# Seven products in place of eight for the down units of the first and last MLP quarter, with three order edges and other PSUM banks

## The chip, the core and the metric

The kernel runs on one core of a Trainium2 chip. The metric is device time in microseconds for one execution of the whole block. PE is TensorE, DVE VectorE, ACT ScalarE, POOL GpSimd and SP the engine that issues most transfers.

## The reference

One decoder block over a sequence of 512 rows of width 1024, all in float32. A mixer (an SSD scan and a causal pooling, merged by sigmoid gates) comes first; the change is in the MLP behind it, and in the last weights of the merge:

```python
h = rmsnorm(x, norm_mix_w[i]) * (1.0 + scale_m) + shift_m
x = x + gate_m * hybrid_mixer(h, ...)          # ends in (g_ssd * y_ssd + g_pool * y_pool) @ w_out
h = rmsnorm(x, norm_mlp_w[i]) * (1.0 + scale_f) + shift_f
x = x + gate_f * (jnp.square(jax.nn.relu(h @ w_up[i])) @ w_down[i])
return rmsnorm(x, norm_final_w)
```

`w_up` is 1024 x 4096, `w_down` 4096 x 1024.

## The kernel before, in words

**Numbers.** Every operand of a large product is split into a high and a low part in fp32r (`two`, L834: ACT copies the high part, DVE takes the difference), and a product is three matmuls: high x high, high x low, low x high (`mm3` for plain products, L156 to L158; `product` for the others, L873). Weights arrive as raw float32 by a transfer from SP into one of four raw buffers `RL` and are split into the nine buffers `HL`. PE takes the weights as the stationary operand, 128 x 128 at a time, and the activations as the moving one.

**Transposed work.** Activations lie as 8 tiles of 128 features by 512 rows. A unit of weights gives one output tile: 8 x 3 = 24 matmuls over 512 columns, into one PSUM bank.

**Quarters.** The 4096 hidden features are worked in four quarters `q` of 8 tiles. In each, up units make 8 tiles `us` (relu, square, split: `activated`, L1067), and down units add 8 output tiles to the residual `x1` (L1174 or L1190). Order of the jobs: the four first up units of quarter 0 as one job (`up_first`, halves of 256 columns), four single up units (`up_plain`), then for each quarter a job of two down units `down_plain(q, (0, 1))`, the other six, and the up units of the next quarter. The very last job, `last_down`, has three down units and the final norm.

**Pairs.** Two units that share their moving operand are a 2 x 2 block product, and `Pair` (L875) does it with seven block products over 256 columns instead of eight (Strassen's scheme in Winograd's form): 7 x 12 = 84 matmuls of 256 columns in place of 2 x 24 of 512. It needs sums of weight blocks and sums of the moving blocks. The weights: `fetch` loads `ya`, `yb` and `y4` by SP and adds two more blocks by accumulating transfers from POOL (L890, L891); `prepare` and `prepare_rest` make two further sums in a tile `z` by DVE (L904 needs `ya`, L907 needs `yb`) and split all of it: S1 and A11 from `ya`, S2 and S4 from `z`, S3 and A12 from `yb`, A22 from `y4`. The moving operand: `sums` (L839) makes the four T tiles from two activation tiles, in place of nothing for plain units; `SQ` lists the quarters whose activations get them, and which therefore have pairs for down units. Before, `SQ = (1,2)`: quarter 0 has six single down units, quarter 3 two, and their weights come as plain units.

A pair's steps on PE: `lead` or `first` (A11 x B11, with A12 x B21 ahead in `lead`), `open` (S1 x T1 into the bank of c12; ACT copies it aside as `s5`, L952), `middle` (S2 x T2; DVE adds `s5` into c12, L964), `third` (S3 x T3 into the same columns as S2 x T2, so only after L964 has read them; DVE makes the other half of the result, L971), `close` (S4 x B22 into c12, A22 x T4 into the bank `ac`). For an up pair, `close` has ACT read both halves of c (L1072 over 256 columns, twice), and then `ac` (L1072 over 512 columns).

**Banks.** PSUM has eight banks. Single units take from `PU` (banks 2 and 3), pairs take `ac` in turn from `AC` (banks 0 and 1) and c11 and c12 from `BE` (banks 4 to 7). Taking and giving back is first in, first out.

**Order.** `run_jobs` (L985) lists the work: before a job runs, the next job's weights are prepared (`ahead`), and the first part of a pair is opened inside the pair before it. `pump` issues the fetches for as long as raw buffers (and, for a pair, one of two buffers `Y4`) are free. The build then writes each engine's order from that list: an instruction in `tc.high_priority()` is taken earlier when it is ready, others as they become ready by the build's own estimate of time; at run time each engine goes through its order. `tc.issue_after(x)` makes what it encloses come behind `x` on the engine of `x`, with no other wait.

**In front of the MLP.** The merge ends with eight gate units; for each ACT does a sigmoid (L728), DVE two steps (L730, L731), and `split` (L126, L127) makes the operand of the units of `w_out` that follow. The weights of `up_first` are converted by ACT whenever they are there.

Of the kernel before, what the change touches and what calls it, by code (L numbers as in the profile page):

```python
# [13 lines left out]
T = 512  # L14
# [48 lines left out]
def block_kernel(tc, xp, crow, arow, par, adaT, wstart, wz, wx, wpool_in, wgate, wpw, wbs, wbp, wout, wup, wdn, out):  # L63
# [3 lines left out]
    with (  # L67
# [53 lines left out]
        done = [None]  # L121

        def split(src):

            hi, lo = S.get(F32R), S.get(F32R)
            act.copy(hi, src)  # L126
            done[0] = dve.tensor_tensor(lo, src, hi.bitcast(F32), ALU.subtract)  # L127
            return hi, lo
# [596 lines left out]
        for j in range(8):  # L725
            gs = F.get()
            ps = unit(wgate[j], h)
            last = act.activation(gs, ps, AF.Sigmoid)  # L728
            PU.put(ps)
            dve.tensor_tensor(gs, gs, acc[j], ALU.mult)  # L730
            dve.tensor_tensor(gs, gs, merged[j], ALU.add)  # L731
            S.put(acc[j])
            F.put(merged[j])
            mg.append(split(gs))
            F.put(gs)
            if rows:
                ada_next()
        free(h)
# [91 lines left out]
        U.free = U.free[:2]  # L830
        spare, ut = [], []
# [43 lines left out]
        class Pair:  # L875
# [24 lines left out]
            def prepare(self):  # L900
                ya, yb = self.y
                self.a, self.left = {}, {}
                z = Z.get()
                dve.tensor_tensor(z[:, :T], ya[:, :T], ya[:, T:], ALU.add)  # L904
                self.keep(ya, "S1", "A11")
                RL.put(ya)
                dve.tensor_tensor(z[:, T:], z[:, :T], yb[:, T:], ALU.add)  # L907
                self.keep(z, "S2", "S4")
                Z.put(z)
# [51 lines left out]
            def middle(self):  # L961
                self.mul(self.ac[:, :H], "S2", "T2")
                with tc.high_priority():
                    dve.tensor_tensor(self.c12, self.ac[:, :H], self.s5, ALU.add)  # L964
                if not self.led:
                    self.mul(self.c11, "A12", "B21")

            def third(self):
                self.mul(self.ac[:, :H], "S3", "T3")
                with tc.high_priority():  # L970
                    dve.tensor_tensor(self.ac[:, H:], self.ac[:, :H], self.s5, ALU.add)  # L971
                U5.put(self.s5)
# [12 lines left out]
        def run_jobs(jobs):  # L985
# [10 lines left out]
            for n, job in enumerate(jobs):  # L996
# [6 lines left out]

                def rest():
                    if isinstance(after, Pair):
                        after.prepare_rest()
                    pump()

                if isinstance(job, Pair):
# [11 lines left out]
                    job.middle()  # L1021
                    if isinstance(after, Pair):
# [4 lines left out]
                else:  # L1027
# [3 lines left out]
                    ahead()  # L1031
                    job.run()
                    rest()
                    if job.after:
                        job.after()

# [28 lines left out]
        us, h2t, hb, ub, held = [], [], {}, {}, []  # L1065

# [53 lines left out]
        def h2_sums():  # L1120
# [10 lines left out]
            spare.extend([S.get(), S.get()])  # L1131
            U.free += [2, 3]
            quarter = [raws[i // 4][:, i % 4, :].bitcast(F32R) for i in range(8)]
            wide = [HI0.get(F32R) for _ in range(2)]
            quarter += [wide[i // 2][:, i % 2 * T:i % 2 * T + T] for i in range(4)]
            for p in range(3):
                ut.append([quarter[4 * p:4 * p + 2], quarter[4 * p + 2:4 * p + 4]])
# [24 lines left out]
        def down_plain(q, js):  # L1162

            def f(w):
# [3 lines left out]
                ps = [PU.get() for _ in js]  # L1168
                n = len(js)
                order = [(k, i) for k in range(6) for i in range(n)] + [(k, i) for i in range(n) for k in (6, 7)]  # L1170
# [6 lines left out]
                PU.put(*ps)  # L1177
# [37 lines left out]
        SQ = (1,2)  # L1215
        jobs = [Plain([Unit(wup[i // 2], i % 2, HI0 if i < 2 else None) for i in range(4)], up_first)]
        jobs += [up_plain(p, i) for p in (2, 3) for i in range(2)]
        jobs[-1].after = h2_sums
# [88 lines left out]
```

## Time and profile before

| | |
|---|---|
| median of 3 runs | 965.71 us (964.55 to 969.83) |
| profiled execution | 964.54 us |
| its span | 962.8 us |
| granted TensorE clock, mean | 0.998 |
| PE busy | 944.3 us, 98% |
| weight loads busy (PEld) | 808.8 us, 84% |
| DVE, ACT, POOL busy | 682.1, 524.0, 121.1 us |
| transfers | 143.43 MB, 149 GB/s over the span |

The span runs from the first to the last instruction; the time lies around it. Matmuls overlap in the records, each from its start to its modelled end, so a busy PE says less than the distance from one start to the next. A row of the timeline gives start, duration, engine, line, operation, tiles (written<-read), how many, and in brackets the idle time before it with what ended it.

### The profile page before, as it was taken

To read this page: it belongs to the slowest core of one execution; us is meant where nothing else is said; L and a number is where in the kernel's file an instruction comes from. 1 tells how busy PE (TensorE), PEld (TensorE's weight loads), DVE (VectorE), ACT (ScalarE), POOL (GpSimd) and SP (SyncE) were. 2 spreads that over 40 slices of the span, in tenths; PEclk is the share of its full clock that TensorE was granted. 3 is DMA by queue.
4 is the path that set the end of the run, shared out by engine and by line. 5 is a ranking of instruction groups with operands and counts; after the bars stand their busy time and mean duration, and the time that the engine had idled before them with its cause. 6 is when DMAs were issued, how large, how long until landed. Compare 5 with 4: busy or idle time off the path is not lost.

```text
span 962.8 us, 13939 instructions
## 1 busy us (share of the span) xinstructions
PE 944.3 (98%) x5347; PEld 808.8 (84%) x5347; DVE 682.1 (71%) x1034; ACT 524.0 (54%) x855; POOL 121.1 (13%) x127
## 2 busy tenths in 40 slices
PE   8999999999999999999999999999999999999996
PEld 4877888888888888788888878997899999899986
DVE  7978868467766787977576574783458878877544
ACT  6479975657528542563312452684147638646633
POOL 0102321220212132300000000000111120111000
PEclk9999999999999999999999999999999999999999
DMA  9846334433253334546578454042556676677402
GB/s 364 303 133 188 125 98 121 131 110 110 79 159 114 98 99 132 158 153 205 181 255 273 130 198 130 23 132 86 133 126 173 147 192 150 179 176 158 148 1 88
DMA packets 69350, 143.43 MB, mean 149 GB/s; under 512 B 5346, under 2 KB 30178, under 8 KB 69283
## 3 DMA queue, kind: packets, MB, share of 16 engines
q1 hardware_dynamic: 64096, 133.09, 43.4%
q0 software_dynamic: 5184, 9.44, 6.6%
q8 instruction: 42, 0.69, 0.3%
q14 instruction: 26, 0.20, 0.1%
q10 hardware_dynamic: 2, 0.00, 0.0%
HBM read 140.29 MB, written 2.23 MB: 148 GB/s over the span
## 4 chain that ended last, share of the span: by engine, by line
PE 79%; DVE 10%; ACT 4%; DMA 4%; issue 2%; POOL 0%; SPq 0%; DVEq 0%; ACTq 0%; POOLq 0%
PE ps L156 19%; PE ps L157 19%; PE ps L158 19%; PE ps L873 14%; PE ps L328 4%; DVE d L147 1%; PE ps L549 1%; DMA d<-cs_d 1%; DVE s L127 1%; DMA d<-wup 1%; DMA d<-wdn 1%; PE ps L529 1%; DVE pad L631 1%; DVE d L172 1%; ACT d L146 1%
## 5 line engine op out<-in xcount | busy, mean ns | idle before, releaser
L156 PE MATMUL ps<-s,d 128*128 128x512 f32 (+1 forms) x984 | 375.1, 381 | 2.4 <-ACT s L126 0.9
L157 PE MATMUL ps<-s,d 128*128 128x512 f32 (+1 forms) x984 | 371.3, 377 | 0.2 <-DVE s L127 0.2
L158 PE MATMUL ps<-s,d 128*128 128x512 f32 (+1 forms) x984 | 371.3, 378 | 0.0
L156 PEld LDWEIGHTS ps<-s,d 128*128 128x128 f32 x984 | 184.6, 188 | 41.2 <-issue 2.4
L158 PEld LDWEIGHTS ps<-s,d 128*128 128x128 f32 x984 | 184.7, 188 | 34.7 <-issue 0.2
L157 PEld LDWEIGHTS ps<-s,d 128*128 128x128 f32 x984 | 184.8, 188 | 33.7 <-DVE s L127 0.5
L147 DVE TENSOR_TENSOR d<-d,d 128x1024 fp32r<-128x1024 f32 x88 | 112.7, 1281 | 61.4 <-ACT d L146 56.4
L146 ACT CAST d<-d 128x1024 fp32r<-128x1024 f32 x88 | 92.0, 1046 | 114.7 <-PE ps L157 74.1
L837 DVE TENSOR_TENSOR d<-d,d 128x1024 fp32r<-128x1024 f32 x82 | 99.6, 1223 | 63.8 <-PE ps L157 36.3
L873 PE MATMUL ps<-s,d 128*128 128x256 f32 x1134 | 139.7, 280 | 2.5 <-DVE ps L964 2.5
L873 PEld LDWEIGHTS ps<-s,d 128*128 128x128 f32 x1134 | 136.2, 188 | 3.4 <-DVE ps L964 3.1
L836 ACT CAST d<-d 128x1024 fp32r<-128x1024 f32 x82 | 85.7, 1049 | 79.6 <-PE ps L158 55.5
L172 DVE CUSTOM_DVE_ANT_0 d<-d,d,par_t 128x1024 f32<-128x1024 f32 x32 | 41.7, 1306 | 27.4 <-DMA d<-adaT 27.4
L890 POOL DMA_DIRECT2D d<-wup x12 | 10.6, 881 | 289.4 <-DMA d<-wup 277.9
L499 ACT ACTIVATE d<-d,ncs 128x128 f32<-128x128 f32 x128 | 39.9, 391 | 4.1 <-POOL d L495 4.0
L328 PE MATMUL ps<-s,d 128*128 128x512 f32 x168 | 40.2, 392 | 1.9 <-ACT s L316 1.9
L397 DVE SCALAR_TENSOR_TENSOR s<-ps,par_t,s 128x511 f32<-128x511 f32 (+2 forms) x54 | 39.7, 742 | 0.3
L328 PEld LDWEIGHTS ps<-s,d 128*128 128x128 f32 x168 | 31.4, 188 | 9.6 <-ACT s L316 2.4
L126 ACT CAST s<-s 128x512 fp32r<-128x512 f32 x32 | 19.7, 619 | 31.2 <-POOL s L511 18.8
L495 POOL TENSOR_SCALAR_AFFINE_SELECT d<-d 128x1024 f32<-128x1024 f32 x16 | 18.2, 1139 | 87.9 <-ACT cd L492 39.9
L127 DVE TENSOR_TENSOR s<-s,s 128x512 fp32r<-128x512 f32 x32 | 25.7, 806 | 4.5 <-ACT s L126 4.3
L511 POOL TENSOR_TENSOR s<-s,dec 128x512 f32<-128x512 f32 x12 | 14.8, 1234 | 90.0 <-issue 55.2
(230 smaller groups left out, 1126.5 us busy)
## 6 DMA issues: line engine op xcount, KB each, us to landing
d<-adaT SPq DMA_DIRECT2D x32, 512.0 KB, 4.1
d<-wup SPq DMA_DIRECT2D x32, 512.0 KB, 5.1
d<-wdn SPq DMA_DIRECT2D x32, 512.0 KB, 4.7
d<-wx SPq DMA_DIRECT2D x18, 512.0 KB, 3.6
d<-cs_d SPq DMA_DIRECT2D x16, 512.0 KB, 6.1
d<-wbs SPq DMA_DIRECT2D x16, 512.0 KB, 3.5
d<-wgate SPq DMA_DIRECT2D x16, 512.0 KB, 4.3
d<-wz SPq DMA_DIRECT2D x15, 512.0 KB, 3.5
```

The lines of the kernel that those rows point to most:

```text
L146: act.copy(hi[:, :w], r[:, a:a + w])
L147: (low or dve).tensor_tensor(lo[:, :w], r[:, a:a + w], hi[:, :w].bitcast(F32), ALU.subtract)
L156: pe.matmul(ps, whi, xhi[:, t0:t1], start=start, stop=False)
L157: pe.matmul(ps, whi, xlo[:, t0:t1], start=False, stop=False)
L158: pe.matmul(ps, wlo, xhi[:, t0:t1], start=False, stop=stop)
L172: dve.tensor_tensor_reduce(r, r, cbc, 1.0, col("b_ada", j), ALU.mult, ALU.add, mod[:, j:j + 1])
L328: pe.matmul(first[u], w[u][i // 2], h[k][i % 2], start=k == 0 and i == 0, stop=k == 7 and i == 2)
L397: dve.scalar_tensor_tensor(t[:, sh:], ps[:, :T - sh], w(3 - sh), t[:, sh:], ALU.mult, ALU.add)
L499: act.activation(m[:, i, :], m[:, i, :], AF.Exp, bias=ncs[:, c, g * HG + i:g * HG + i + 1])
L836: act.copy(dst[0], src)
L837: dve.tensor_tensor(dst[1], src, dst[0].bitcast(F32), ALU.subtract)
L873: pe.matmul(ps, x, y, start=start and m == 0 and i == 0, stop=m == 3 and i == 2, skip_group_check=True)
```

## The change

Quarters 0 and 3, whose down units were single, get pairs; `SQ` now holds all four: three pairs (output tiles 2 to 7) in quarter 0, one (tiles 2 and 3) in quarter 3. The buffers for the T tiles of quarter 0 are set up from the start (`ut`, `u_sums`), and `pump` runs once more after a job with an `after`, so that the fetch of the first pair can be listed once `h2_sums` has given back `Y4`. Two edges: DVE's second half of `z` comes behind the last addition of the pair at work (`mids`, L964 or L971 at that time; for a plain job, of the pair before it), and the conversion of the first up units' weights comes behind ACT's last copy in the merge (`gated`). A job of two down units takes its two banks from `AC` instead of `PU`.

```diff
-        done = [None]
+        done = [None, None]
...
-            act.copy(hi, src)
+            done[1] = act.copy(hi, src)
             done[0] = dve.tensor_tensor(lo, src, hi.bitcast(F32), ALU.subtract)
...
+        gated = done[1]
         free(h)
...
-        U.free = U.free[:2]
-        spare, ut = [], []
+        spare = [S.get(), S.get()]
+        ut = [[[raws[p][:, 2 * i + k, :].bitcast(F32R) for k in range(2)] for i in range(2)] for p in range(2)]
...
             def prepare(self):
-                ya, yb = self.y
+                ya = self.y[0]
                 self.a, self.left = {}, {}
                 z = Z.get()
                 dve.tensor_tensor(z[:, :T], ya[:, :T], ya[:, T:], ALU.add)
                 self.keep(ya, "S1", "A11")
                 RL.put(ya)
-                dve.tensor_tensor(z[:, T:], z[:, :T], yb[:, T:], ALU.add)
+                self.z = z
+
+            def prepare_more(self):
+                z, yb = self.z, self.y[1]
+                with tc.issue_after(mids[-1].ins) if mids else nullcontext():
+                    dve.tensor_tensor(z[:, T:], z[:, :T], yb[:, T:], ALU.add)
                 self.keep(z, "S2", "S4")
                 Z.put(z)
...
-                    dve.tensor_tensor(self.c12, self.ac[:, :H], self.s5, ALU.add)
+                    mids.append(dve.tensor_tensor(self.c12, self.ac[:, :H], self.s5, ALU.add))
...
-                    dve.tensor_tensor(self.ac[:, H:], self.ac[:, :H], self.s5, ALU.add)
+                    mids.append(dve.tensor_tensor(self.ac[:, H:], self.ac[:, :H], self.s5, ALU.add))
...
+                def more():
+                    if isinstance(after, Pair):
+                        after.prepare_more()
...
                     job.middle()
+                    more()
                     if isinstance(after, Pair):
                         after.open()
                     job.third()
...
                     ahead()
+                    more()
                     job.run()
                     rest()
                     if job.after:
                         job.after()
+                        pump()
...
-            spare.extend([S.get(), S.get()])
-            U.free += [2, 3]
-            quarter = [raws[i // 4][:, i % 4, :].bitcast(F32R) for i in range(8)]
+
+        def u_sums():
+
             wide = [HI0.get(F32R) for _ in range(2)]
-            quarter += [wide[i // 2][:, i % 2 * T:i % 2 * T + T] for i in range(4)]
-            for p in range(3):
-                ut.append([quarter[4 * p:4 * p + 2], quarter[4 * p + 2:4 * p + 4]])
+            ut.append([[w[:, :T], w[:, T:]] for w in wide])
...
-                ps = [PU.get() for _ in js]
                 n = len(js)
+                at = AC if n == 2 else PU
+                ps = [at.get() for _ in js]
...
-                PU.put(*ps)
+                at.put(*ps)
...
-        SQ = (1,2)
-        jobs = [Plain([Unit(wup[i // 2], i % 2, HI0 if i < 2 else None) for i in range(4)], up_first)]
+        SQ = (0,1,2,3)
+        jobs = [Plain([Unit(wup[i // 2], i % 2, HI0 if i < 2 else None, gated) for i in range(4)], up_first)]
         jobs += [up_plain(p, i) for p in (2, 3) for i in range(2)]
-        jobs[-1].after = h2_sums
+        jobs[0].after, jobs[-1].after = u_sums, h2_sums
```

More of the change, by code (lines that the diff above doesn't have):

```diff
@@ L1065, in block_kernel @@
         us, h2t, hb, ub, held = [], [], {}, {}, []
+        mids = []
         def activated(q, p, i, ps, sign):
```

## The prediction

> **What bounds the kernel now.** I read the page first, then the busy times by stretch, then the waits of PE, then the single engines around each wait.
>
> ```profile
> span 962.8 us, 13939 instructions
> PE 79%; DVE 10%; ACT 4%; DMA 4%; issue 2%; POOL 0%; SPq 0%; DVEq 0%; ACTq 0%; POOLq 0%
> ```
>
> PE carries 79% of the chain that ended last, so what counts is how many products PE issues and where it stands still. The sum below is made against the profiled execution: 964.54 us around a span of 962.8. That is the lowest of the runs shown (964.55) and 1.17 us under their median of 965.71.
>
> Two kinds of MLP work stand side by side in the stretches (busy time of each engine, instructions in brackets):
>
> ```profile
> core 0: us, PE busy (x) PEld busy (x) DVE busy (x) ACT busy (x) POOL busy (x), PEclk, DMA share, GB/s
> 676.96:687.94 10.98, 10.98 (x49) 9.02 (x48) 4.92 (x6) 2.10 (x2) 1.74 (x2) 1.00 0.68 145
> 773.66:783.56 9.90, 9.90 (x87) 9.90 (x86) 7.57 (x11) 4.41 (x6) 1.64 (x3) 1.00 0.78 187
> 637.00:660.00 23.00, 23.00 (x106) 19.01 (x106) 13.04 (x15) 18.35 (x29) 0.00 (x0) 1.00 0.59 181
> 660.00:671.00 11.00, 11.00 (x49) 8.90 (x48) 3.05 (x3) 3.70 (x5) 0.00 (x0) 1.00 0.16 48
> ```
>
> The first row is two plain down units of the first quarter (2 x 24 products over 512 columns), the second one pair of the second quarter (84 products over 256 columns) between two other pairs. Both run with PE full and the granted clock at 1.00. The third row is the four plain up units, the fourth the first plain down job; both matter for the sums below.
>
> Where PE stands still after 560 us (us in total, times, longest):
>
> ```profile
> PE ps L873 <- DVE ps L964: 2.5, 3, 1.6
> PE ps L156 <- ACT s L126: 0.9, 1, 0.9
> PE ps L156 <- DVE xs L1174: 0.4, 1, 0.4
> ```
>
> These are idle times after the modelled end of a product, and the true loss is larger, as one of the three waits for L964 shows:
>
> ```profile
> 739.75 0.63 PE L873 MATMUL ps<-s,d 128*128 128x256 f32 x4
> 741.10 0.50 PE L873 MATMUL ps<-s,d 128*128 128x256 f32 x2 [0.72 <-DVE ps L964]
> ```
>
> In a full stretch such products start every 9.90 / 84 = 0.118 us, so the fourth started at 740.10 and the next at 741.10: 1.00 - 0.12 = 0.88 lost, where the view says 0.72. I add 0.16 to each wait.
>
> **The change, part by part.**
>
> *Four pairs in place of eight plain units* (`SQ` now holds all quarters: three pairs in quarter 0, one in quarter 3). 10.98 - 9.90 = 1.08 us each, 4.3 us in all, if the pairs run as those of the second quarter do. The cover: a pair takes 7.57 us of DVE and 4.41 of ACT in 9.90, so both keep room. Its two accumulating transfers go through POOL, which issues nothing from 637 to 671; SP gets three loads for a pair where two units had two. Quarters 0 and 3 get a first pair behind a plain job, which they did not have; the start of such a pair (756.45: four products in 0.75, not 0.63) costs 0.1, so 0.2 in all.
>
> ```profile
> 756.45 0.75 PE L873 MATMUL ps<-s,d 128*128 128x256 f32 x4
> 743.88 0.62 ACT L836 CAST d<-pad 128x512 fp32r<-128x512 f32 x1
> 661.35 0.59 ACT L1072 ACTIVATE pad<-ps 128x512 f32<-128x512 f32 x1
> 661.97 0.63 ACT L1073 ACTIVATE pad<-pad 128x512 f32<-128x512 f32 x1
> ```
>
> *The sums of the activations, now in quarter 0 too.* Each of four pairs of activations adds four half-width DVE steps, two DVE differences and two ACT casts (0.62 each as at 743.88). DVE is busy 13.04 of 23.00 us there and 3.05 of the next 11: it has room. ACT is busy 18.35 of 23.00 while PE does the up units, and each of these needs a PU bank back that ACT reads (661.35). Four casts for the first two pairs come ahead of those reads: they cost 0 if the 4.65 idle us take them, and 4 x 0.62 = 2.5 if all four stand before a read that PE waits for. I take 0.5, nearer to the idle row. The last pair's sums come after 662 and have until the first pair's third product, some 10 us later.
>
> *`gated`: the first MLP weights are converted only behind the last split of the merge.*
>
> ```profile
> 570.76 1.05 ACT L836 CAST d<-d 128x1024 fp32r<-128x1024 f32 x1 [0.68 <-DMA d<-wup]
> 571.72 0.59 ACT L728 ACTIVATE sz<-ps 128x512 f32<-128x512 f32 x1
> 572.33 1.28 ACT L740 ACT_TABLE_LOAD   x1
> 573.79 0.62 ACT L126 CAST s<-sz 128x512 fp32r<-128x512 f32 x1 [0.18 <-DVE sz L731]
> ```
>
> A conversion of up weights waits for its transfer and holds the sigmoid of the last gate unit behind it; the split at 573.79 ends 0.9 us of PE idle (the second wait above, 1.05 with the overlap). The conversion moves behind; the sigmoid moves up by the 0.68 of waiting and most of the 1.05 of the cast, more than the 1.05 lost. Gain 1.05. What waits for the moved conversions is PE at about 614, and the raw buffers that they free: 40 us of cover.
>
> *`mids`: the second half of z comes behind the additions in PSUM.*
>
> ```profile
> 740.01 0.69 DVE L907 TENSOR_TENSOR d<-d,d 128x512 f32<-128x512 f32 x1 [1.48 <-DMA d<-wdn]
> 740.62 0.43 DVE L964 TENSOR_TENSOR ps<-ps,pad 128x256 f32<-128x256 f32 x1
> 822.22 0.69 DVE L907 TENSOR_TENSOR d<-d,d 128x512 f32<-128x512 f32 x1 [1.50 <-DMA d<-wdn]
> 822.83 0.42 DVE L964 TENSOR_TENSOR ps<-ps,pad 128x256 f32<-128x256 f32 x1
> 883.98 0.69 DVE L907 TENSOR_TENSOR d<-d,d 128x512 f32<-128x512 f32 x1 [2.23 <-DMA d<-wup]
> ```
>
> In all three waits of PE for L964, DVE sat in L907 until weights landed, with the addition that PE needs queued behind. Put behind the addition, the wait touches nobody: the sums S2 and S4 that it feeds are used a whole job later. Gain 2.5 + 3 x 0.16 = 3.0.
>
> *The AC banks for the down job of two units.* The wait for L1174 at 671 goes (0.4 + 0.16 = 0.5), since a pair comes next and opens in another bank. But in quarters 1 to 3 the job now takes as its second bank the one that the last up pair has just closed, and PE must wait until ACT has read it (L1072). The nearest row for this is the bank wait at the start of the first down job, behind the last plain up unit:
>
> ```profile
> 660.20 0.39 PE L156 MATMUL ps<-s,d 128*128 128x512 f32 x1
> 662.03 0.46 PE L156 MATMUL ps<-s,d 128*128 128x512 f32 x1
> ```
>
> There ACT read the bank at 661.35 to 661.94, and PE filled the time with eight products for its first bank (660.20 to 662.03) and lost under 0.1. That is the low end. The high end is the queue of ACT as it stands now at these places; it is the first rival. I take the low end, 0.1 for each of three: it is the same job, with the same kind of read in front of its second bank, in the only place where this wait exists today.
>
> Each wait that goes also takes the slow product behind it (0.50 for two at 741.10, against 0.63 - 2 x 0.118 = 0.39): 5 x 0.1 = 0.5.
>
> Sum: 4.3 + 1.05 + 3.0 + 0.5 + 0.5 = 9.35 gained; 0.2 + 0.5 + 0.3 = 1.0 paid. 964.54 - 8.35 = 956.2 us.
>
> **The rivals.**
>
> *The bank wait eats the gain.* Today's queue of ACT at the end of the up pairs of quarters 1 and 2:
>
> ```profile
> 744.41 0.38 ACT L1072 ACTIVATE s<-ps 128x256 f32<-128x256 f32 x1
> 746.50 1.05 ACT L836 CAST d<-d 128x1024 fp32r<-128x1024 f32 x1 [1.72 <-DMA d<-wdn]
> 747.99 0.58 ACT L1072 ACTIVATE s<-ps 128x512 f32<-128x512 f32 x1
> 828.15 1.05 ACT L836 CAST d<-d 128x1024 fp32r<-128x1024 f32 x1 [1.16 <-DMA d<-wdn]
> 829.63 0.58 ACT L1072 ACTIVATE s<-ps 128x512 f32<-128x512 f32 x1
> 745.45 0.40 PE L156 MATMUL ps<-s,d 128*128 128x512 f32 x1
> 827.65 0.39 PE L156 MATMUL ps<-s,d 128*128 128x512 f32 x1
> ```
>
> The conversion of the next pair's weights waits for its transfer in front of the read of the closed bank, which ends at 748.57 and 830.21. PE now starts the down job at 745.45 and 827.65 in other banks; with the waits above gone it would be there at 744.5 and 825.8. Eight products cover 1.83, so PE would lose 748.57 - 744.5 - 1.83 = 2.2 and 2.6 us, and about as much in quarter 3, which gets a pair to convert at the same place: 7.2 in place of my 0.3, 963.1 us. With three products as cover (0.69) it is 10.6 and 966.5. Against it: this order came about while nobody waited for that read, each engine's order is written anew with the edges, and one of the two conversions in front moves behind with z. For it: the order is the same in both quarters, and no edge of the change is set on ACT here. This is the rival that I fear most.
>
> On the way PE and ACT could get around such a wait, the Trainium skill ("TensorE: Matmul & The Clock Gate", queue depths) says that ACT and DVE take their queues strictly in order and that PE pulls only weight loads ahead, with its matmuls in program order. By that nothing at run time repairs a bad order, and the trace agrees: DVE held L964 behind L907 at 740.01, ACT the read behind the conversion at 746.50.
>
> *The pairs save nothing*, because loading weights bounds them: in the stretch of the pair PEld is busy for all of its 9.90 us, in the plain one for 9.02 of 10.98. If the four new pairs took a plain pair's 10.98, the time would be 956.2 + 4.3 = 960.5. Against it: the pairs that are there run at 9.90 with just these loads, so it gets next to no chance.
> The same page of the Trainium skill (sustained throughput) gives about 81 ns for a matmul over 128 columns and 131 over 512; by that 84 products take at least 6.8 us and 48 take 6.3, an estimate by which each pair would lose 0.5 and the sum be 962.5. The trace doesn't agree: 10.98 / 48 is 229 ns and 9.90 / 84 is 118.
>
> *Slower: the weights of the first pairs come too late.* A pair's raw halves are loaded by SP and then added to by POOL:
>
> ```profile
> 640.91 0.38 SPq L1049 DMA_DIRECT2D d<-wdn  x1
> 671.15 0.33 SPq L886 DMA_DIRECT2D d<-wup  x1
> 679.92 0.69 DVE L904 TENSOR_TENSOR d<-d 128x512 f32<-128x512 f32 x1 [6.37 <-DMA d<-wup]
> ```
>
> From the load's issue to the first use of the sum, 671.15 to 679.92 are 8.8 us, against a pair of 9.9. The first pair starts at about 671; its loads must be out by about 660. For the kernel to be slower by 0.5% the 8.35 and another 4.8 must be lost, so the first pair's loads would have to go out at about 673, behind the down job, as those of the first up pair do now (671.15). Then 970 us or more. Against it: the raw buffers come free early in this stretch; the fourth unit's load now goes out at 640.91, and the pair's takes that place.
>
> **How the numbers follow.** My forecast, 956.2 us, gets 0.53; the bank wait 0.36 (963.1 us; in a tenth of these only one of three places is hit, about 958.5); pairs that save nothing 0.02 (960.5); late weights 0.07; 0.02 is left for slower in other ways. About 0.5%, 4.8 us, is what a measurement of this kernel can tell from no change. Faster: 0.53 + 0.04 = 0.57; same: 0.34; slower: 0.09. The forecast's own range is 954.7 (nothing paid but the late starts, 9.35 - 0.2 = 9.15 gained, and 0.7 for the spread of its terms) to 958.5; for 8 in 10 it has to reach over most of the bank wait: 954.5 to 964.5.
>
> **What would show it.** Right: 84 products in 9.9 us in each of the four new pairs; no PE wait at 573, none for L964; the read of the closed bank (L1072 over 512) within 1.8 us of the start of each down job. Wrong: PE waiting for L1072 at the second bank of the down jobs of quarters 1 to 3, behind a conversion that waits for d<-wdn; PE waiting for L1072 among the up units of quarter 0 (ACT too full); L904 or L907 of the first pair waiting for a transfer past 671.

## The result and the profile after

The changed kernel takes 963.12 us (median of 20 runs, 960.32 to 966.87), the kernel before 966.00 beside it (20 runs). The ratio is 0.9973, with a 95% interval of 0.9962 to 0.9984: 2.6 us or 0.27% faster by the ratio (2.9 between the medians). The interval stays below 1, but the gain is smaller than the half per cent that the prediction took as the least a measurement can tell from no change. The forecast was 956.2, so 6.9 us of its gain are missing.

The profiled execution took 964.88 us, 1.8 over the median, around a span of 963.2. From the page of the changed kernel, its head and the two groups of products that wait most (busy us, mean ns | idle us before them and what ended most of it):

```profile
span 963.2 us, 14354 instructions
PE 942.0 (98%) x5491; PEld 812.7 (84%) x5491; DVE 718.7 (75%) x1116; ACT 540.1 (56%) x891; POOL 128.1 (13%) x135
L156 PE MATMUL ps<-s,d 128*128 128x512 f32 (+1 forms) x920 | 350.8, 382 | 5.3 <-ACT pad L1086 4.1
L874 PE MATMUL ps<-s,d 128*128 128x256 f32 x1314 | 163.4, 280 | 2.5 <-DVE d L838 2.5
```

The lines have moved: the addition L964 is now L970, L971 is L977, the evictions L1072 and L1174 are L1086 and L1187, a conversion's two halves are L837 (ACT) and L838 (DVE). The three waits of before that the change aims at (L964 2.5 us, L126 0.9, L1174 0.4) are gone from PE's waits after 560 us. Two others stand in their place (us in total, times, longest):

```profile
PE ps L156 <- ACT pad L1086: 4.1, 3, 1.6
PE ps L874 <- DVE d L838: 2.5, 3, 1.7
```

*The new pairs run as forecast.* Two of quarter 0, by stretches:

```profile
681.00:690.90 9.90, 9.90 (x86) 9.90 (x85) 9.13 (x13) 4.50 (x6) 1.74 (x2) 1.00 0.69 179
690.90:700.80 9.90, 9.90 (x87) 9.90 (x85) 7.97 (x12) 4.50 (x6) 1.72 (x2) 1.00 0.79 188
```

PE is full for 9.90 us, with the counts and the clock of the pair shown before (x87, 1.00). The one pair of quarter 3 is spread among products of the last job (920.41 to 931.54, all 84 products recorded), so its own length can't be read.

*The first new wait* comes three times, at 735, 819 and 902. PE and ACT at the first of them:

```profile
734.37 0.63 PE L874 MATMUL ps<-s,d 128*128 128x256 f32 x4
736.59 0.50 PE L156 MATMUL ps<-s,d 128*128 128x512 f32 x1 [1.60 <-ACT pad L1086]
736.93 0.28 PE L874 MATMUL ps<-s,d 128*128 128x256 f32 x1
734.48 1.05 ACT L837 CAST d<-d 128x1024 fp32r<-128x1024 f32 x1 [1.70 <-DMA d<-wdn]
735.43 0.62 ACT L1087 ACTIVATE pad<-pad 128x512 f32<-128x512 f32 x1
735.97 0.58 ACT L1086 ACTIVATE pad<-ps 128x512 f32<-128x512 f32 x1
```

A single product of the down job (L156) stands between products of the last up pair (L874). It stands there because of the edge on z: the kernel without that edge (no_z_edge below) has no such product inside the pair. That the build puts it there to fill a wait that it expects for the addition L970 is my reading, not shown. Its bank is one of AC's, and ACT reads that bank (735.97) only behind a conversion that stood 1.70 us waiting for weights. PE issues nothing in between: with the four products of the row starting 0.118 apart the last began at 734.72, the next at 736.59, 1.87 where 0.12 is normal. The three places cost 1.76, 1.22 and 1.63 over the pitch (the normal distance from one start to the next, 0.118 us for 256 columns and 0.229 for 512), 4.6 us in all, and a slow product behind each.

*The second new wait* comes at 671, 753 and 837, 0.39, 1.87 and 0.76 over the pitch. The one at 753, on PE, ACT, DVE and POOL:

```profile
753.41 0.40 PE L874 MATMUL ps<-s,d 128*128 128x256 f32 x2
755.51 0.74 PE L874 MATMUL ps<-s,d 128*128 128x256 f32 x4 [1.71 <-DVE d L838]
750.72 1.05 ACT L837 CAST d<-d 128x1024 fp32r<-128x1024 f32 x1 [4.58 <-DMA d<-wdn]
752.63 1.09 DVE L838 TENSOR_TENSOR s<-s,s 128x256 fp32r<-128x256 f32 x3 [3.77 <-ACT s L837]
754.24 1.22 DVE L838 TENSOR_TENSOR d<-d,d 128x1024 fp32r<-128x1024 f32 x1
741.75 0.86 POOL L892 DMA_DIRECT2D d<-wdn  x1 [0.44 <-DVE pad L844]
```

The third product of the first down pair needs the low part of A12, a half of yb. POOL issues yb's accumulating transfer at 741.75 and ACT can convert only at 750.72, 9.0 us later (the trace has it land at 750.70); DVE takes the low part last, until 755.46, behind splits of the sums. Together the two waits make 4.6 + 3.0 = 7.6 us of lost pitch.

### The profile page after: what moved, and what is told of

The parts are those of the page before. It is cut to its first block, busy times and chain, and to the rows that moved or that the text cites. A ratio compares the mean times of both kernels' runs of the same rounds, so it can differ in the third digit from the quotient of the medians.

```text
span 963.2 us, 14354 instructions
## 1 busy us (share of the span) xinstructions
PE 942.0 (98%) x5491; PEld 812.7 (84%) x5491; DVE 718.7 (75%) x1116; ACT 540.1 (56%) x891; POOL 128.1 (13%) x135
## 4 chain that ended last, share of the span: by engine, by line
PE 76%; DVE 11%; DMA 6%; ACT 4%; issue 2%; POOL 0%; SPq 0%; DVEq 0%; POOLq 0%; ACTq 0%
PE ps L874 20%; PE ps L156 16%; PE ps L157 16%; PE ps L158 16%; PE ps L328 4%; DMA d<-wdn 4%; DVE d L147 2%; PE ps L549 1%; DVE s L397 1%; DVE d L838 1%; DVE s L127 1%; PE ps L529 1%; DMA d<-wgate 1%; PE ps L503 1%; DVE d L172 1%
## 5 line engine op out<-in xcount | busy, mean ns | idle before, releaser
L156 PE MATMUL ps<-s,d 128*128 128x512 f32 (+1 forms) x920 | 350.8, 382 | 5.3 <-ACT pad L1086 4.1
L157 PE MATMUL ps<-s,d 128*128 128x512 f32 (+1 forms) x920 | 346.5, 377 | 0.2 <-DVE s L127 0.2
L158 PE MATMUL ps<-s,d 128*128 128x512 f32 (+1 forms) x920 | 346.0, 377 | 0.0
L156 PEld LDWEIGHTS ps<-s,d 128*128 128x128 f32 x920 | 172.7, 188 | 41.8 <-ACT pad L1086 4.7
L158 PEld LDWEIGHTS ps<-s,d 128*128 128x128 f32 x920 | 172.7, 188 | 32.0 <-issue 0.2
L157 PEld LDWEIGHTS ps<-s,d 128*128 128x128 f32 x920 | 172.8, 188 | 31.1 <-DVE s L127 0.7
L874 PE MATMUL ps<-s,d 128*128 128x256 f32 x1314 | 163.4, 280 | 2.5 <-DVE d L838 2.5
L874 PEld LDWEIGHTS ps<-s,d 128*128 128x128 f32 x1314 | 158.8, 188 | 3.6 <-DVE d L838 3.1
L147 DVE TENSOR_TENSOR d<-d,d 128x1024 fp32r<-128x1024 f32 x88 | 112.9, 1283 | 61.9 <-ACT d L146 57.0
L146 ACT CAST d<-d 128x1024 fp32r<-128x1024 f32 x88 | 92.0, 1046 | 116.0 <-PE ps L157 75.1
L837 ACT CAST d<-d 128x1024 fp32r<-128x1024 f32 x86 | 89.8, 1048 | 68.3 <-PE ps L874 24.2
L838 DVE TENSOR_TENSOR d<-d,d 128x1024 fp32r<-128x1024 f32 x86 | 104.6, 1220 | 20.1 <-ACT d L837 9.0
L891 POOL DMA_DIRECT2D d<-wdn x10 | 8.8, 883 | 306.2 <-DMA d<-wdn 255.1
L328 PEld LDWEIGHTS ps<-s,d 128*128 128x128 f32 x168 | 31.4, 188 | 9.6 <-ACT s L316 2.4
L126 ACT CAST s<-s 128x512 fp32r<-128x512 f32 x32 | 19.7, 619 | 31.2 <-POOL s L511 18.7
L838 DVE TENSOR_TENSOR s<-s,s 128x512 fp32r<-128x512 f32 (+1 forms) x38 | 21.2, 573 | 7.7 <-ACT s L837 7.5
```

What stands on the lines that cost most here:

```text
L146: act.copy(hi[:, :w], r[:, a:a + w])
L147: (low or dve).tensor_tensor(lo[:, :w], r[:, a:a + w], hi[:, :w].bitcast(F32), ALU.subtract)
L156: pe.matmul(ps, whi, xhi[:, t0:t1], start=start, stop=False)
L157: pe.matmul(ps, whi, xlo[:, t0:t1], start=False, stop=False)
L158: pe.matmul(ps, wlo, xhi[:, t0:t1], start=False, stop=stop)
L328: pe.matmul(first[u], w[u][i // 2], h[k][i % 2], start=k == 0 and i == 0, stop=k == 7 and i == 2)
```

## The experiments

Three theories. **A**: the bank of the down job (AC in place of PU) makes the first wait. **B**: the weights of the pairs come late, and whatever PE waits for stands behind them; **B1**, since their transfers share the DMA engines with the next load, **B2**, since yb's buffer comes free late for the load after next. **C**, the rival: the added pairs fill ACT and DVE, so waits only move. Times are medians, from five rounds beside the kernel before; the ratio is to that kernel. Each profile is one execution, and some lie off their median. The change has two order edges, the one on z and the one at the gated stage; the title's "three" is a slip.

| kernel | us | ratio [95%] |
|---|---|---|
| changed kernel | 963.1 | 0.9973 [0.9962, 0.9984] |
| pu_banks | 970.2 | 1.0047 [1.0029, 1.0066] |
| no_z_edge | 969.0 | 1.0036 [1.0020, 1.0052] |
| pu_no_z | 973.3 | 1.0077 [1.0047, 1.0108] |
| pairs_only | 975.1 | 1.0085 [1.0054, 1.0115] |
| ac_q0 | 963.0 | 0.9967 [0.9949, 0.9985] |
| no_accum | 959.2 | 0.9931 [0.9906, 0.9955] |
| sq12 | 964.8 | 0.9987 [0.9968, 1.0007] |
| edges_only | 966.3 | 1.0003 [0.9984, 1.0022] |
| sq12_no_accum | 962.0 | 0.9964 [0.9945, 0.9983] |
| ac_q0_no_accum | 956.9 | 0.9906 [0.9886, 0.9926] |
| hold_ya | 963.4 | 0.9975 [0.9957, 0.9994] |
| yb_first | 961.9 | 0.9956 [0.9938, 0.9974] |
| yb_first_q0 | 961.1 | 0.9947 [0.9926, 0.9967] |
| yb_q0_hold | 959.7 | 0.9932 [0.9908, 0.9956] |
| z_third_q0 | 975.3 | 1.0098 [1.0072, 1.0124] |

**pu_banks**: the down job's banks from PU again.

```diff
-                at = AC if n == 2 else PU
+                at = PU
```

> The down job of two units takes its banks from PU again (one line of the change undone; AC is no longer used there); all else as in the changed kernel. Theory A, bank wait: in the changed kernel the first product of this job sits inside the last up pair in PE's order, its bank comes from AC, and PE loses 1.87, 1.35 and 1.75 us of pitch around it in quarters 1 to 3 (L156 behind ACT L1086, 4.1 us idle in the groups). With banks from PU the product finds a free bank: these waits go, 4.9 us less, and the span is about 958 against 963 of the changed kernel, 0.992 of the kernel before. The wait of 0.5 at 671 may come back, then 958.5. Theory B, late weights: the three waits of L874 for DVE L838 (0.50, 1.98, 0.87 us over the pitch) have another cause and stay, 2.5 us idle in the groups. Theory C, the four added pairs crowd ACT and DVE so that the waits only move: the time stays within 1 us of the changed kernel, 0.997, and PE's idle time shows up at other lines.

Measured: 970.2, 7 us slower than the changed kernel, where A said 5 faster. PE's waits after 560 us:

```profile
PE ps L156 <- ACT s L1086: 5.1, 1, 5.1
PE ps L874 <- DVE ps L977: 3.1, 3, 1.2
PE ps L874 <- DVE d L838: 1.8, 3, 1.1
```

The first of them on PE and ACT, in quarter 0:

```profile
659.88 0.39 PE L157 MATMUL ps<-s,d 128*128 128x512 f32 x1
665.38 0.79 PE L156 MATMUL ps<-s,d 128*128 128x512 f32 x1 [5.11 <-ACT s L1086]
662.23 0.62 ACT L837 CAST d<-pad 128x512 fp32r<-128x512 f32 x1 [0.61 <-DVE pad L845]
664.43 0.41 ACT L837 CAST s<-s 128x256 fp32r<-128x256 f32 x1 [1.58 <-DVE s L842]
664.74 0.59 ACT L1086 ACTIVATE s<-ps 128x512 f32<-128x512 f32 x1
```

And the stretch behind it (us, busy time and count of PE, PEld, DVE, ACT and POOL, granted clock, DMA share, GB/s):

```profile
664.00:668.00 4.00, 2.62 (x6) 2.14 (x7) 3.36 (x7) 3.29 (x6) 0.87 (x1) 0.50 0.32 118
```

ACT reads the last up unit's bank at 664.74 only, behind the casts of the sums that quarter 0 now needs, which wait for DVE in turn. In the changed kernel this read comes as late, at 664.47, but there the job has AC's banks and PE goes on without it. So the edit that I priced at 0.5 us holds off a stall of 5.27 over the pitch, and behind it 9 products 0.43 apart in place of 0.23, with the clock granted at 0.50 (2.3 more with the two beside them). The three waits at AC's bank did go, but PE then waits 3.1 for L977. So A holds for where the wait stood and not for the time, and C holds in quarter 0: there the added sums do crowd ACT.

**no_z_edge**: AC kept, no edge on the second half of z.

```diff
-                with tc.issue_after(mids[-1].ins) if mids else nullcontext():
+                with nullcontext():
```

> The edge on the second half of z is left out; the down job of two units keeps its banks from AC. Theory A, that it takes both the edge (which puts one down product into the last up pair) and the AC bank to lose the 4.9 us: no product of the down job stands inside the pair, so no wait of L156 for ACT L1086 at the job's first bank. In its place the waits of the kernel before come back, PE L874 behind DVE at the last additions of the pair, 0.4 to 0.6 each in six places, 3.0 us in all. Sum: 963.1 - 4.9 + 3.0 = 961.2, 0.995 of the kernel before, if the second bank is free in time. The prediction's rival: PE then stands at the second bank of the job, behind ACT's conversion that waits for d<-wdn, 2.2 to 2.6 us in three quarters: 968, 1.002. Theory C: within 1 us of the changed kernel, 0.997.

Measured: 969.0, slower than all three had it. There is no product of the down job inside the up pair, as expected, but PE waits for L970 in five places (before the change 2.5 us in three):

```profile
PE ps L874 <- DVE ps L970: 8.8, 5, 3.5
```

With pairs in every quarter the edge is worth 5.9 us here (969.0 - 963.1), where 3.0 was forecast.

**pu_no_z** (both undone) and **pairs_only** (as well no edge at the gated stage):

> Both undone: banks from PU and no edge on the second half of z; the four added pairs and the edge at the gated stage stay. Theory A: no wait at the bank of the down job, but the waits for the additions of the pair come back (3.0 us): 958.3 + 3.0 = 961.3, 0.995. Against the kernel with banks from PU alone this gives the worth of the edge by itself: 3 us. Theory C (the pairs crowd ACT and DVE): no faster than the changed kernel, 0.997 or above.

> The four added pairs with their buffers and nothing else: banks from PU, no edge on z, no edge at the gated stage. The prediction's term for the pairs, 4 x 1.08 = 4.3 us less 0.2 to 0.5 paid: about 4 us under the kernel before, 0.996; PE runs each added pair at 118 ns a product. Theory C: 0.999 to 1.001, the pairs' own conversions eat what they save. With the kernel above it (which has the edge at the gated stage too) the difference is that edge, 0.9 us.

Measured: 973.3 and 975.1. Both have the stall at the first down job (4.9 and 4.8 us) and the waits for L970 (8.8 and 6.7); pairs_only has the wait of before for L126 (1.0), which pu_no_z has not: that edge does what it should. So the pairs by themselves cost 9 us: their saving needs both the edge and the banks, since the kernels with one of the two (pu_banks, no_z_edge) are 4 and 3 us slower than the kernel before. With PU's banks the edge is worth 3.1 us (973.3 - 970.2), with AC's 5.9. The 0.995 and 0.996 that I expected of the two kernels both missed by over 1%.

**ac_q0**: AC in quarter 0 alone.

```diff
-                at = AC if n == 2 else PU
+                at = AC if n == 2 and q == 0 else PU
```

> The changed kernel with the banks of the two-unit down job from AC in quarter 0 alone, and from PU in quarters 1 to 3. From the kernel with PU everywhere: its loss stood in quarter 0 (PE idle 5.1 us at 660 for ACT's read, then 9 products at 427 ns), while its three later stretches, from one set of pairs to the next, were 1.4, 1.5 and 0.8 us shorter than in the changed kernel. If the bank is the cause in each place, this takes the better of both: 963.1 - 3.7 = 959.4, 0.993 of the kernel before. A part of the first 1.4 came with a pitch of 113 in place of 118 ns; without it 1.9 us remain, 961.2 and 0.995. If the waits only move to the pair's last additions (L977, 1.0 to 1.4 each in the PU kernel), within 0.5 us of the changed kernel, 0.997.

Measured: 963.0, the rival's value. The waits move:

```profile
PE ps L874 <- DVE d L838: 3.1, 3, 1.8
PE ps L874 <- DVE ps L977: 3.0, 3, 1.4
```

This profile is of the slowest execution, 968.0, 5 us over the median. But its waits are 7.1 us over the pitch where the changed kernel has 7.6, so theory A alone falls: with late weights the bank decides where PE stands in quarters 1 to 3, not how long.

**no_accum**: no accumulating transfers.

```diff
-                    pool.dma_start(ya[:, :T], w[:, 3 * T:], accum_op=ALU.add)
-                    pool.dma_start(yb[:, :T], w[:, T:2 * T], accum_op=ALU.add)
```

> The changed kernel without the accumulating transfers of the pairs (the added halves of the weights are left out of the sums ya and yb, so this computes something else; every matmul, conversion and other transfer stays). Theory B, the weights of the pairs arrive late: yb lands 8.8 us after its accumulating transfer is issued at 741.75, ACT's conversion stands 4.6 us waiting for it, and what PE waits for (the read of the bank at L1086, 4.9 us over the pitch, and the low part of A12 at L838, 3.4 us) stands behind such a conversion. With the weights there some 6 us earlier both go: 963.1 - 8.3 = 954.8, 0.988 of the kernel before. Theory C, ACT and DVE are too full with the added pairs: the waits stay, 961 to 963, 0.996.

Measured: 959.2, 3.9 faster than the changed kernel, about half of what B said. (The 4.9 and 3.4 of the expectation are whole distances from start to start; over the pitch they are 4.6 and 3.0.) Most of what stays is a wait at the *second* bank of the down job:

```profile
PE ps L156 <- ACT s L1084: 1.9, 3, 0.8
```

It costs 0.71, 0.78 and 0.93 over the pitch in quarters 1 to 3. In the first of them ACT reads the bank at 743.01, behind casts of the sums and a conversion that itself had stood 0.62 us for its plain load. One wait at the first bank is left too, 0.54 at 896. The run takes away the traffic of these transfers together with their lateness, and can't tell one from the other.

**ac_q0_no_accum**: the last two edits together.

> The changed kernel without the accumulating transfers, banks from AC in quarter 0 alone. Without these transfers PE still waited 0.71, 0.78 and 0.93 us over the pitch at the second bank of the down job (for the read at L1084, as that kernel numbers it), 2.4 in all. Theory A, the bank from AC: with PU these go, 959.2 - 2.4 = 956.8, 0.991 of the kernel before. If PE then stands at another line in their place, as with the transfers (963.0 against 963.1): 959, 0.993.

Measured: 956.9 where 956.8 was expected. From 560 us on no wait of PE over 0.3 us is left but the one in the last norm that the kernel before has too; the busy times from the page, and the whole list of PE's waits there:

```profile
PE 943.0 (98%) x5491; PEld 813.7 (85%) x5491; DVE 719.9 (75%) x1116; ACT 540.6 (56%) x891; POOL 89.6 (9%) x91
```

```profile
PE ps L778 <- ACT s L1164: 0.6, 1, 0.6
```

DVE and ACT do the same work as in the changed kernel (1116 and 891 instructions) and PE no longer waits for them: C falls as a limit of its own. The stretches say it too. From the last product of one quarter's first down job to that of the next, the changed kernel takes 82.9, 83.8 and 83.2 us, this one 80.7 each time; that is 7.7 less in all, and the two waits were 7.6. Without the transfers the choice of bank is worth 2.3 us by the medians (the two intervals overlap), and with them nothing.

**sq12** (pairs in quarters 1 and 2 alone, `SQ = (1,2)`, with the transfers) and **sq12_no_accum** (without):

> The changed kernel with the half-width pairs in quarters 1 and 2 alone, as before the change; the edges and the AC banks stay. The prediction's term for the four added pairs is 4 x 1.08 = 4.3 us less 0.2 to 0.5 for the sums' late start: 963.1 + 4 = 967, 1.001 of the kernel before. The waits at the start of the down job in quarter 3 and at the first A12 of quarter 0 (1.63 and 0.39) belong to the added pairs; if they vanish with them, 965, 0.999. Theory C, that the added pairs save nothing because of their conversions: 963, 0.997.

> The changed kernel without the accumulating transfers (the added halves left out of ya and yb) and with pairs in quarters 1 and 2 alone. It measures what the four added pairs save where no pair's weights come late: the kernel with all pairs and no accumulating transfers took 959.2. The prediction's term, 4 x 1.08 = 4.3: 963.5, 0.998 of the kernel before. If the added pairs save only the 1.7 that they save with the transfers (964.8 - 963.1), for a cause other than late weights: 960.9, 0.995.

Measured: 964.8 and 962.0. The four added pairs save 1.7 us with the transfers and 2.8 without. The kernel with all pairs has one more wait at the second bank (the 0.93 of quarter 3); with it the second figure is 3.7, and with the 0.54 at the first bank 4.2, against the 4.1 to 4.3 forecast. Both differences have intervals of 2 to 3 us either way, so neither is clear of noise.

**edges_only**: the kernel before with the two edges (and, as in the change, the second half of z listed later).

> The kernel before with the two edges alone (the second half of z behind the addition at L970, the first conversions of quarter 0 behind the gated stage): pairs in quarters 1 and 2, banks from PU, the order of the sums as before. The prediction's terms: 3.0 for the edge on z and 1.05 for the other: 966 - 4 = 962, 0.996. Theory B, the late yb holds DVE a step later instead, at the addition of L977 behind z (1.0 to 1.4 in the kernel with PU banks, here in two quarters): 964 to 965, 0.998.

Measured: 966.3, no gain over the kernel before (965.7 beside it). The waits after 560 us:

```profile
PE ps L874 <- DVE ps L977: 1.9, 2, 1.0
PE ps L874 <- DVE d L838: 1.5, 2, 1.3
PE ps L156 <- DVE xs L1187: 0.4, 1, 0.4
```

The 2.5 us of L964 and the 0.9 of L126 are gone, and 3.4 stand at the next addition and at A12 (over the pitch 3.0 and 1.05 gone, 2.3 and 1.9 come). The edge on z doesn't remove the wait for the weights, it passes it on.

**hold_ya**: an order edge on SP, a pair's load of ya behind the y4 load of the pair before.

```diff
+                    with tc.issue_after(y4s[-1].ins) if y4s else nullcontext():
+                        sp.dma_start(ya, w[:, :1024])
...
+                    y4s.append(sp.dma_start(self.y4, w[:, 3 * T:]))
```

> The changed kernel with one more order edge on SP: a pair's load of ya behind the load of the pair before's y4 (PE's order is unchanged). At 740.91 that load goes out half a microsecond ahead of two accumulating transfers, which then take 8.8 us to land; alone they took 5.9. Theory B1, they are late since they share the engines with the next load: the load goes out at 745 or later, the transfers land some 2 us earlier, the waits at L838 (3.4 us) go down by 2 or more, and the time to 961, 0.995. Theory B2, they are late since they are issued late (the buffer of yb comes free late): nothing gained, 963, or the next pair's ya is late in its turn and the time is above 964.

Measured: 963.4. It doesn't decide B1: at the place in question the load went out at 741.24 (740.91 in the changed kernel), since the y4 load it waits behind was out long ago. The transfer issued at 741.72 landed at 748.92, after 7.2 us in place of 9.0, and of the wait at A12 little is left in the profile:

```profile
PE ps L874 <- DVE d L838: 0.3, 1, 0.3
```

Its three stretches from down job to down job are 2.6 us shorter together than the changed kernel's, which would speak for B1; the median shows nothing of it.

**yb_first**: yb converted ahead of z.

```diff
-                self.keep(z, "S2", "S4")
-                Z.put(z)
+                self.keep(yb, "S3", "A12")
+                RL.put(yb)
...
-                yb = self.y[1]
-                self.keep(yb, "S3", "A12")
-                RL.put(yb)
+                self.keep(self.z, "S2", "S4")
+                Z.put(self.z)
```

> The changed kernel with yb converted ahead of z, so that its buffer comes free some 2.3 us earlier (one conversion by ACT and one by DVE) for the load of the pair after next. Theory B2, the buffer of yb sets the time of the next yb: its load and its accumulating transfer go out about 2 us earlier, the waits at L838 and at L1086 shrink by 3 or 4 us, 959.5, 0.993. The price: S2 and S4 come that much later; if PE waits for them in the middle of a pair, up to 1 us in each of 23 places, and the time is 965 or more.

Measured: 961.9. yb's transfer for the first down pair of quarter 1 is issued at 737.93 and lands at 744.21, 6.5 us earlier than in the changed kernel, and the waits for A12 are gone. So far B2 holds: when the buffer of yb comes free decides when its transfer goes out. But 959.5 was expected; the 1.3 us that came (by the medians) are not clear of noise, since the intervals of the two kernels overlap. What is left:

```profile
PE ps L874 <- DVE ps L969: 3.0, 3, 1.6
PE ps L156 <- ACT s L1085: 2.2, 2, 2.0
```

**yb_first_q0** and **yb_q0_hold** add the bank of ac_q0, the second also the edge of hold_ya:

> yb converted ahead of z, and the banks of the two-unit down job from AC in quarter 0 alone. With yb converted first PE still waited at the second bank of the down job (L1085) 0.24, 0.35 and 2.16 us over the pitch in quarters 1 to 3. Theory A: the bank from PU takes these away as it did without the accumulating transfers (959.2 to 956.9): 961.9 - 2.5 = 959.4, 0.993. If PE then stands at the last additions in their place, as with yb converted last (963.0 against 963.1): 962, 0.996.

> The same, with the load of a pair's ya behind the load of the pair before's y4 on SP. By itself that order took the waits at L838 from 3.1 to 0.6 us in the profile and left the median where it was. If the late transfer is what is left, 1 to 2 us under the kernel without it, 958 and 0.992; if not, the same as that.

Measured: 961.1 and 959.7. The bank wait goes, and PE waits 3.7 and 4.0 us for the first addition of the last up pair in three places. The second kernel beats both kernels of this study: its interval, 0.9908 to 0.9956, lies below that of the changed kernel. Whether the edge on SP has a part in that isn't settled; the two intervals overlap. What is left in it, on PE and DVE:

```profile
739.26 0.51 PE L874 MATMUL ps<-s,d 128*128 128x256 f32 x2 [1.19 <-DVE ps L970]
738.17 0.69 DVE L838 TENSOR_TENSOR s<-pad,s 128x512 fp32r<-128x512 f32 x1 [1.85 <-ACT s L837]
738.78 0.43 DVE L970 TENSOR_TENSOR ps<-ps,pad 128x256 f32<-128x256 f32 x1
```

Again the addition stands behind a split that waits for ACT.

**z_third_q0**: the second half of z asked for behind L977, AC in quarter 0.

```diff
                     job.middle()
-                    more()
                     if isinstance(after, Pair):
                         after.open()
                     job.third()
+                    more()
```

> The changed kernel with banks from AC in quarter 0 alone and the second half of z, with its conversions, asked for behind the pair's second addition (L977) in place of the first (L970). With banks from PU in quarters 1 to 3 PE waited for L977 1.56, 0.91 and 1.03 us over the pitch. If the z sum and its conversions stand in front of it on DVE, these 3.5 go: 963 - 3.5 = 959.5, 0.993. If DVE is only late since ACT stands at a conversion that waits for its transfer, nothing changes, 963; and S2 and S4 may come late in their turn, 965.

Measured: 975.3 (the profile is of the slowest execution, 978.6). PE's new order mixes products of the down job and of the pairs beside it, and PE waits for conversions that now come too late:

```profile
PE ps L874 <- ACT d L837: 4.1, 3, 1.5
PE ps L874 <- DVE d L838: 2.9, 3, 1.4
PE ps L156 <- ACT s L837: 2.7, 4, 1.2
PE ps L157 <- DVE s L838: 2.1, 4, 1.0
```

The wait for L977 is gone and 11.8 us stand elsewhere; the 965 that I had set for this case was 10 us too mild.

## Why the prediction was wrong

- *Pairs, 4.3*: held by the trace, with 9.90 us each where one can be read. The kernels without the transfers give 2.8 to 4.2, within 3 us either way.
- *`gated`, 1.05*: held. At 573 two products start 0.36 and 0.34 after the ones before them, 0.13 and 0.11 over the pitch where it had been 1.05 and 0.11; the next stage starts 0.8 earlier.
- *`mids`, 3.0*: **failed**. "Put behind the addition, the wait touches nobody" is wrong. The wait for L964 did go, but what DVE had waited for, the sum yb, also holds ACT's queue and then A12 and L977. edges_only gained nothing. (Beside the new pairs the edge is worth 3.1 to 5.9 us, since without it the waits for L970 are longer than before the change; the forecast's 3.0 was not taken from that.) I followed the sum z to its use, "a whole job later", and not the other instructions that wait for the same transfer.
- *AC banks, 0.5 gained and 0.3 paid*: **failed both ways**. The gain was under-sized: without them quarter 0 loses 7 us (pu_banks). The price was 4.6 in place of 0.3. Of the two ends that I had, 0.1 and 2.2 to 2.6 a place, I took the low one, from the only place where such a read stands in the way today. The read there had no conversion waiting for weights in front of it, the reads here had, and that row was quoted in the rival. With PU's banks in these three quarters (ac_q0) PE stood about as long at L977 and A12, so the 4.6 can't be put down to the bank alone.
- *ACT crowd among the sums of quarter 0, 0.5 paid*: the crowd came, and 5.1 us of it, but the AC banks keep PE out of it. Each of the two steps was priced without the other.
- *Late weights of yb*: no term at all. They cost 3.0 over the pitch at A12, and 3.9 in all by no_accum. I held a loop of 8.8 us against a pair of 9.9 and called it cover enough for the first pair, but asked it of quarter 0 only. Behind the plain job the loop is longer: the accumulating transfer alone takes 9 us there.
- The sum: 956.2 + 4.6 (bank) + 3.0 (A12) is 963.8; the profiled execution had 964.88. The rest is small: 0.7 for the slow products behind the six waits and 0.7 for the last stage's half-width products, 5 ns slower each than in the profile of before (on this below), against 0.8 of crowd and second bank that weren't paid; 0.5 is left unexplained. The profiled execution lies 1.8 over the median, so this adds up one execution, not the median.

The first rival gave 963.1, the time that came. That is half luck. Its mechanism is there, a bank of AC behind ACT's conversion that waits for d<-wdn, but at the first bank and for one product that the order edge had moved into the pair; at the second bank, where I looked for it, PE lost 0.1. Its 7.2 for this alone are 4.6, and late A12 fills the rest. The prediction's sign for "wrong" (waits at the second bank) would not have found it; the sign for a first pair waiting on its transfer comes nearest. The range, 954.5 to 964.5, holds the time because it reached over that rival.

ac_q0_no_accum gives the forecast its due: all 5491 products and every conversion, 956.9 us. The arithmetic of the pairs was right. Of the 6.9 us missing, 3.9 came back without the accumulating transfers and 2.3 more with the bank; 0.7 is left.

What stays open is why yb's transfer takes 9 us there. From 640 us on the changed kernel issues 44 accumulating transfers, and most land after 4.0 to 5.6 us. The eight that took over 6 us were each issued within 2 us of another one (yb's at 741.75 behind one at 740.45, 9.0 and 8.8). So beside B1 there is a rival that no run tried: two accumulating transfers in each other's way. Some that were issued as close took 4 to 5 us, so closeness alone doesn't do it. How much of yb_q0_hold's gain each of its edits brings is open too.

## What to carry to other kernels

An order edge that lets one instruction pass a wait doesn't shorten the wait: list everything on every engine that waits for the same transfer, and see who is next. Price edits that touch the same buffers together; here one edit's 0.5 was 7 beside another. A kernel that leaves the suspected transfer out shows in one run how much of a miss hangs on it, lateness and traffic together.

## What the runs showed of the hardware

*A stall of PE can halve its clock afterwards.* pairs_only, the stretch with the stall and the next two (columns as above; the granted clock is the third from the right):

```profile
744.35:747.70 3.35, 1.23 (x10) 1.02 (x9) 2.04 (x4) 2.64 (x6) 0.87 (x1) 0.99 0.78 274
747.70:750.90 3.20, 3.20 (x17) 3.20 (x16) 2.98 (x7) 1.56 (x2) 1.72 (x2) 0.50 0.80 175
750.90:754.00 3.10, 3.10 (x22) 2.86 (x21) 2.44 (x5) 2.58 (x5) 0.00 (x0) 0.98 0.99 172
```

Behind 2.4 us without a product, the clock is granted at 0.50 for 3.2 us; the products start 213 ns apart in place of 118, and the stall costs 1.4 us more. In the traces of this study, from 560 us on, none of 28 single stalls of 1.2 to 2.0 us (start to start) had this, and 12 of 15 of 2.1 us and more had it; z_third_q0, where stalls come in clusters, isn't counted. So here the price of a wait mostly jumped at about 2.1 us, but not always: stalls of 2.22, 2.38 and 3.11 us had no slow time behind them. The waits of the changed kernel, 1.98 at most, stay just below. The Trainium skill ("TensorE: Matmul & The Clock Gate", "What's actually happening") gives half the clock after an idle window of about 3.4 us, in windows that run freely. The 0.50 and the length of the slow time agree; stalls of 2.1 to 2.8 us were often enough here, less than the window.

*The same products run at one of two paces.* A stretch of quarter 0 in pu_banks, beside that of the changed kernel above (690.90 to 700.80, x87):

```profile
690.90:700.80 9.90, 9.90 (x90) 9.90 (x89) 8.34 (x12) 4.51 (x6) 1.74 (x2) 1.00 0.86 203
```

Three more products in the same time at the same clock: they start 113 ns apart here and 118 there, for whole stretches, and the pace can change at a short hiccup of PE (in pu_banks at 722, where two recorded starts lie 0.22 apart). Over the 590 products from one down job to the next that is 2.8 us, as much as the whole effect of the change; so single profiles a few us apart were not read here as a gain or a loss. What sets the pace was not tried, so it isn't shown either that it falls by chance.
